# A pooling kernel whose engines are ordered by its own semaphores, with the framework's closing barriers placed after the first loads

## The chip, the cores and the metric

The kernel runs on one core of one Trainium2 chip. The metric is the device time of one execution in microseconds (us), the median of several runs. Five engines take part in a program, each with a queue of instructions of its own: TensorE (PE), VectorE (DVE), ScalarE (ACT), GpSimd (POOL) and SyncE (SP). The core's 16 DMA engines move data between the chip's memory (HBM) and the on-chip memory with its 128 partitions. Engines wait for one another, and for transfers, only through semaphores.

## What is computed

The reference is an adaptive average pool in one dimension. The input is float32 of 32 x 256 x 4096, the output 32 x 256 x 256, and each output is the mean of 16 neighbouring inputs:

```python
for i in range(output_size):
    start = int(i * length / output_size)
    end = int((i + 1) * length / output_size)
    result[:, :, i] = np.mean(x[:, :, start:end], axis=-1)
```

So 134.22 MB are read, 8.39 MB are written, and there is little arithmetic on each number.

## The kernel before

Batch and channel together make 8192 rows. A tile has 128 partitions with 4 rows each, so there are 16 tiles; one is 128 x 16384 numbers, 64 KB per partition. The first 15 tiles are cut so that a partition owns 60 rows that follow one another in memory (`x_many`, `o_many`, lines 46 and 47); the last tile has 4 rows per partition (`x_last`, `o_last`, lines 48 and 49).

One loop (line 56) runs over the tiles. Line 64, on SP's queue, loads a tile into one of two buffers (`inpool`, `bufs=2`, line 51). Each tile has 1024 windows of 16 numbers per partition, and two engines share them. POOL (line 67) folds the second 512 windows: it adds the upper 8 numbers of each to the lower 8, in place. DVE sums the first 512 windows whole (line 72) and then the folded ones (line 75). ACT (line 78) multiplies the 1024 sums by 1/16, in place, in the result tile. The results of 15 tiles stay on the chip in `res_many` and go out in one store (line 66), which stands on SP's queue behind the last load; those of the last tile are in `res_last` and go out in three stores (line 84), of 112, 8 and 8 partitions.

No semaphore is written in the kernel. The framework puts them in from the tiles that each instruction reads and writes: POOL and DVE wait for a load, DVE's second sum for POOL's fold, ACT for DVE, load t+2 for DVE's sums of tile t, the stores for ACT. Every transfer is issued by SP, whose queue is followed in order, so that an instruction that waits holds up all behind it.

The framework also frames the program. Line 101 opens it with a barrier over the five engines. Line 115, where the tile context ends, closes it: SP waits for each DMA semaphore (four wait instructions and a drain), then all engines meet in a barrier (each drains, raises a semaphore at POOL, and waits for POOL's release), POOL clears the framework's semaphores, and all engines meet in a second barrier. The profile puts a "q" behind an engine's name where it speaks of the engine's sequencer: SPq L115 is SP's part in this.

Of the kernel before, what the change touches and what calls it, by code (L numbers as in the profile page):

```python
# [1 line left out]

# [4 lines left out]


@with_exitstack
def kernel(  # L10
    ctx: ExitStack,
    tc: tile.TileContext,
    x: bass.AP,
    output_size: int,
    out: bass.AP,
):

    nc = tc.nc
    F32 = mybir.dt.float32
    X = mybir.AxisListType.X

    batch, channels, length = x.shape
    ob, oc, olen = out.shape
    assert ob == batch and oc == channels and olen == output_size
    assert length % output_size == 0
    window = length // output_size  # L30
    hw = window // 2
    inv_w = 1.0 / float(window)

    P = nc.NUM_PARTITIONS
    R = 4
    rows = batch * channels
    assert rows % (P * R) == 0
    ntiles = rows // (P * R)
    many = (ntiles - 1) * R
    cells = R * output_size  # L40
    m = cells // 2
    cols = R * length

    xr = x.rearrange("b c l -> (b c) l")
    orow = out.rearrange("b c o -> (b c) o")
    x_many = xr[0 : P * many, :].rearrange("(p r) l -> p (r l)", p=P, r=many)
    o_many = orow[0 : P * many, :].rearrange("(p r) o -> p (r o)", p=P, r=many)
    x_last = xr[P * many :, :].rearrange("(p r) l -> p (r l)", p=P, r=R)
    o_last = orow[P * many :, :].rearrange("(p r) o -> p (r o)", p=P, r=R)

    inpool = ctx.enter_context(tc.tile_pool(name="inpool", bufs=2))
    respool = ctx.enter_context(tc.tile_pool(name="respool", bufs=1))
    res_many = respool.tile([P, (ntiles - 1) * cells], F32, name="res_many")
    res_last = respool.tile([P, cells], F32, name="res_last")

    for t in range(ntiles):
        last = t == ntiles - 1
        xin = inpool.tile([P, cells, window], F32, name="xin")
        if last:
            res, base, src = res_last, 0, x_last  # L60
        else:
            res, base = res_many, t * cells
            src = x_many[:, t * cols : (t + 1) * cols]
        nc.sync.dma_start(out=xin.rearrange("p o w -> p (o w)"), in_=src)  # L64
        if last:
            nc.sync.dma_start(out=o_many, in_=res_many[:, :])
        nc.gpsimd.tensor_add(  # L67
            out=xin[:, m:cells, 0:hw],
            in0=xin[:, m:cells, 0:hw],
            in1=xin[:, m:cells, hw:window],  # L70
        )
        nc.vector.reduce_sum(  # L72
            out=res[:, base : base + m], in_=xin[:, 0:m, :], axis=X
        )
        nc.vector.reduce_sum(  # L75
            out=res[:, base + m : base + cells], in_=xin[:, m:cells, 0:hw], axis=X
        )
        nc.scalar.mul(  # L78
            out=res[:, base : base + cells],
            in_=res[:, base : base + cells],  # L80
            mul=inv_w,
        )
    for lo, hi in ((0, 112), (112, 120), (120, 128)):
        nc.sync.dma_start(out=o_last[lo:hi, :], in_=res_last[lo:hi, :])


# [1 line left out]
_INS = ['x', 'output_size']  # L88
_OUTS = [((32, 256, 256), 'float32')]

_NUMBERS = {'output_size': 256}


# [26 lines left out]
```

## Time and profile before

| What | Value |
|---|---|
| Time, median of 3 runs | 335.1 us (335.01 to 335.28) |
| Span of the profiled execution, first to last instruction of the program | 333.2 us |
| What lies around that span (335.1 - 333.2) | 1.9 us |
| Instructions in the profile | 160 |
| DVE busy | 209.7 us (63%) |
| POOL busy | 139.7 us (42%) |
| ACT busy | 18.2 us (5%) |

The time of the profiled execution is not listed apart from its span; what lies around the span is therefore taken from the median. It is the runtime's own work before and after the program, and no view of the profile shows it.

Reading: shares of busy time are means over the whole span. The timeline gives starts and durations in us from the span's start. A row of digits cuts the span, or the window asked for, into 40 equal slices, and a digit is the busy share of a slice in tenths (9 is 90% or more); in a short window a DMA packet counts in the slice in which it starts. The view of waits says who waited for whom: total, number of times, longest.

### The profile page before, as it was taken

To read this page: it belongs to the slowest core of one execution; us is meant where nothing else is said; L and a number is where in the kernel's file an instruction comes from. 1 tells how busy PE (TensorE), PEld (TensorE's weight loads), DVE (VectorE), ACT (ScalarE), POOL (GpSimd) and SP (SyncE) were. 2 spreads that over 40 slices of the span, in tenths; PEclk is the share of its full clock that TensorE was granted. 3 is DMA by queue.
4 is the path that set the end of the run, shared out by engine and by line. 5 is a ranking of instruction groups with operands and counts; after the bars stand their busy time and mean duration, and the time that the engine had idled before them with its cause. 6 is when DMAs were issued, how large, how long until landed. Compare 5 with 4: busy or idle time off the path is not lost.

```text
span 333.2 us, 160 instructions
## 1 busy us (share of the span) xinstructions
DVE 209.7 (63%) x32; ACT 18.2 (5%) x17; POOL 139.7 (42%) x20
## 2 busy tenths in 40 slices
DVE  0029396693929569392956839295783929578491
ACT  1000101000010100001010000101010010101001
POOL 0027091642709064370906336090733609073460
DMA  9898989999898989999898989999898989999997
GB/s 378 378 504 378 496 386 464 417 393 488 378 504 378 504 378 488 393 409 472 378 504 378 504 378 480 401 409 472 378 504 378 504 378 480 401 401 480 399 435 299
DMA packets 2608, 142.61 MB, mean 428 GB/s; under 512 B 304, under 2 KB 304, under 8 KB 432
## 3 DMA queue, kind: packets, MB, share of 16 engines
q1 hardware_dynamic: 2608, 142.61, 99.1%
HBM read 134.22 MB, written 8.39 MB: 428 GB/s over the span
## 4 chain that ended last, share of the span: by engine, by line
DMA 66%; POOL 18%; DVE 11%; POOLq 3%; issue 0%; ACT 0%; SPq 0%
DMA xin<-in_x_dram 66%; POOL xin L67 18%; DVE res_many L75 9%; POOLq L115 3%; DVE res_last L75 1%; ACT res_last L78 0%; SPq L64 0%; POOLq L67 0%
## 5 line engine op out<-in xcount | busy, mean ns | idle before, releaser
L67 POOL TENSOR_TENSOR xin<-xin 128x4096 f32<-128x4096 f32 x16 | 139.5, 8718 | 181.9 <-DMA xin<-in_x_dram 181.9
L72 DVE TENSOR_REDUCE res_many<-xin 128x512 f32<-128x8192 f32 x15 | 130.3, 8686 | 107.8 <-DMA xin<-in_x_dram 107.8
L75 DVE TENSOR_REDUCE res_many<-xin 128x512 f32<-128x4096 f32 x15 | 66.3, 4420 | 2.5 <-POOL xin L67 2.3
L78 ACT ACTIVATE res_many<-res_many 128x1024 f32<-128x1024 f32 x15 | 15.8, 1056 | 290.1 <-DVE res_many L75 290.1
L72 DVE TENSOR_REDUCE res_last<-xin 128x512 f32<-128x8192 f32 x1 | 8.7, 8686 | 6.1 <-DMA xin<-in_x_dram 6.1
L75 DVE TENSOR_REDUCE res_last<-xin 128x512 f32<-128x4096 f32 x1 | 4.4, 4420 | 0.2 <-POOL xin L67 0.2
L78 ACT ACTIVATE res_last<-res_last 128x1024 f32<-128x1024 f32 x1 | 1.1, 1056 | 18.3 <-DVE res_last L75 18.3
L78 ACT ACT_TABLE_LOAD x1 | 1.3, 1283 | 0.7 <-PEq L101 0.7
L101 POOL MEMSET const-float32-0.0<- 128x1 f32 x1 | 0.1, 98 | 0.2 <-issue 0.2
L101 POOL MEMSET const-bfloat16-1.0<- 128x1 bf16 x1 | 0.1, 101 | 0.0
L101 POOL MEMSET const-uint8-127<- 128x1 uint8 x1 | 0.1, 101 | 0.0
L101 POOL MEMSET const-float32-1.0<- 128x1 f32 x1 | 0.1, 98 | 0.0
## 6 DMA issues: line engine op xcount, KB each, us to landing
out_dram<-res_many SPq DMA_DIRECT2D x1, 7680.0 KB, 23.0
out_dram<-res_last SPq DMA_DIRECT2D x1, 448.0 KB, 4.8
xin<-in_x_dram SPq DMA_DIRECT2D x16, 25.4
out_dram<-res_last SPq DMA_DIRECT2D x2, 32.0 KB
```

The lines of the kernel that those rows point to most:

```text
L67: nc.gpsimd.tensor_add(out=xin[:, m:cells, 0:hw], in0=xin[:, m:cells, 0:hw], in1=xin[:, m:cells, hw:window],)
L72: nc.vector.reduce_sum(out=res[:, base : base + m], in_=xin[:, 0:m, :], axis=X)
L75: nc.vector.reduce_sum(out=res[:, base + m : base + cells], in_=xin[:, m:cells, 0:hw], axis=X)
L78: nc.scalar.mul(out=res[:, base : base + cells], in_=res[:, base : base + cells], mul=inv_w,)
L101: nc = _bacc.Bacc("TRN2", target_bir_lowering=False, num_devices=1)
L115: with _tile.TileContext(nc) as tc:
```

## The change

The tile pools go. The two load buffers and one result tensor (of the same total size) are allocated directly, and the kernel declares six semaphores: `landed0`, `landed1` for the loads into the two buffers, `folded` for POOL, `summed` for DVE, `scaled` for ACT and `stored` for the stores. The first two loads are issued inside the framework's critical section; directly behind it the kernel closes the tile context itself (`tc.close()`, `tc.compile()`), so that the framework's end of program (two barriers with POOL's clearing between them) comes at this place. All that follows is ordered by the new semaphores. The last tile's results go out in one store of 128 partitions. At the end SP clears five semaphores, waits for both stores, and clears the sixth; no barrier follows.

```diff
-    inpool = ctx.enter_context(tc.tile_pool(name="inpool", bufs=2))
-    respool = ctx.enter_context(tc.tile_pool(name="respool", bufs=1))
-    res_many = respool.tile([P, (ntiles - 1) * cells], F32, name="res_many")
-    res_last = respool.tile([P, cells], F32, name="res_last")
+    nbuf = 2
+    xin = [
+        nc.alloc_sbuf_tensor(f"xin{i}", [P, cells, window], F32, align_bytes=256)
+        for i in range(nbuf)
+    ]
+    res = nc.alloc_sbuf_tensor("res", [P, ntiles * cells], F32, align_bytes=256)
...
+    def load(t):
+        src = x_last if t == ntiles - 1 else x_many[:, t * cols : (t + 1) * cols]
+        dst = xin[t % nbuf][:, :, :].rearrange("p o w -> p (o w)")
+        nc.sync.dma_start(out=dst, in_=src).then_inc(landed[t % nbuf], 16)
...
+    with tc.tile_critical():
+        for t in range(nbuf):
+            load(t)
+    tc.close()
+    tc.compile()
 
     for t in range(ntiles):
...
+        xt = xin[t % nbuf]
+        lo, mid, hi = t * cells, t * cells + m, (t + 1) * cells
+        here = 16 * (t // nbuf + 1)
+
+        nc.gpsimd.wait_ge(landed[t % nbuf], here)
         nc.gpsimd.tensor_add(
...
-        )
+        ).then_inc(folded, 1)
+
+        nc.vector.wait_ge(landed[t % nbuf], here)
+        nc.vector.reduce_sum(out=res[:, lo:mid], in_=xt[:, 0:m, :], axis=X)
+        nc.vector.wait_ge(folded, t + 1)
         nc.vector.reduce_sum(
...
+            out=res[:, mid:hi], in_=xt[:, m:cells, 0:hw], axis=X
+        ).then_inc(summed, 1)
+
+        nc.scalar.wait_ge(summed, t + 1)
         nc.scalar.mul(
...
-    for lo, hi in ((0, 112), (112, 120), (120, 128)):
-        nc.sync.dma_start(out=o_last[lo:hi, :], in_=res_last[lo:hi, :])
+            out=res[:, lo:hi], in_=res[:, lo:hi], mul=inv_w
+        ).then_inc(scaled, 1)
+
+        if t + nbuf < ntiles:
+            nc.sync.wait_ge(summed, t + 1)
+            load(t + nbuf)
+
+    done = (ntiles - 1) * cells
+    nc.sync.wait_ge(scaled, ntiles - 1)
+    nc.sync.dma_start(out=o_many, in_=res[:, 0:done]).then_inc(stored, 16)
+    nc.sync.wait_ge(scaled, ntiles)
+    nc.sync.dma_start(out=o_last, in_=res[:, done:]).then_inc(stored, 16)
+    for s in (*landed, folded, summed, scaled):
+        nc.sync.sem_clear(s)
+    nc.sync.wait_ge(stored, 32)
+    nc.sync.sem_clear(stored)
```

As built, SP's queue holds after the opening barrier: a no-op that raises a semaphore, a branch to the critical section that waits for it, the two loads, four small instructions that leave the critical section, the two closing barriers, the other 14 loads, the two stores, five clears, and the clear of `stored` with its wait. On POOL, DVE and ACT the two barriers stand ahead of the first wait for a load, and their queues end with the last tile's work. Waits that stood as instructions of their own (SP and POOL had one for most tiles) are part of the instruction that waits.

More of the change, by code (lines that the diff above doesn't have):

```diff
@@ L49 @@
     o_last = orow[P * many :, :].rearrange("(p r) o -> p (r o)", p=P, r=R)
-    inpool = ctx.enter_context(tc.tile_pool(name="inpool", bufs=2))
-    respool = ctx.enter_context(tc.tile_pool(name="respool", bufs=1))
-    res_many = respool.tile([P, (ntiles - 1) * cells], F32, name="res_many")
-    res_last = respool.tile([P, cells], F32, name="res_last")
-    for t in range(ntiles):
[L57 to L70, printed above, removed]
-        )
[L72 to L82, printed above, removed]
@@ L83 @@
-    for lo, hi in ((0, 112), (112, 120), (120, 128)):
-        nc.sync.dma_start(out=o_last[lo:hi, :], in_=res_last[lo:hi, :])
+    nbuf = 2
[4 more added lines that the diff above has]
+    res = nc.alloc_sbuf_tensor("res", [P, ntiles * cells], F32, align_bytes=256)
+    landed = [nc.alloc_semaphore(f"landed{i}") for i in range(nbuf)]
+    folded = nc.alloc_semaphore("folded")
+    summed = nc.alloc_semaphore("summed")
@@ new lines @@
+    scaled = nc.alloc_semaphore("scaled")
+    stored = nc.alloc_semaphore("stored")
+    def load(t):
[7 more added lines that the diff above has]
+    tc.compile()
+    for t in range(ntiles):
+        xt = xin[t % nbuf]
+        lo, mid, hi = t * cells, t * cells + m, (t + 1) * cells
+        here = 16 * (t // nbuf + 1)
+        nc.gpsimd.wait_ge(landed[t % nbuf], here)
+        nc.gpsimd.tensor_add(
+            out=xt[:, m:cells, 0:hw],
+            in0=xt[:, m:cells, 0:hw],
+            in1=xt[:, m:cells, hw:window],
+        ).then_inc(folded, 1)
+        nc.vector.wait_ge(landed[t % nbuf], here)
+        nc.vector.reduce_sum(out=res[:, lo:mid], in_=xt[:, 0:m, :], axis=X)
+        nc.vector.wait_ge(folded, t + 1)
+        nc.vector.reduce_sum(
+            out=res[:, mid:hi], in_=xt[:, m:cells, 0:hw], axis=X
+        ).then_inc(summed, 1)
+        nc.scalar.wait_ge(summed, t + 1)
+        nc.scalar.mul(
+            out=res[:, lo:hi], in_=res[:, lo:hi], mul=inv_w
[3 more added lines that the diff above has]
+            load(t + nbuf)
```

## The prediction

> **What bounds the kernel now.** First the page: its DMA rows, its chain, and the groups.
>
> ```profile
> DMA  9898989999898989999898989999898989999997
> q1 hardware_dynamic: 2608, 142.61, 99.1%
> DMA xin<-in_x_dram 66%; POOL xin L67 18%; DVE res_many L75 9%; POOLq L115 3%; DVE res_last L75 1%; ACT res_last L78 0%; SPq L64 0%; POOLq L67 0%
> L67 POOL TENSOR_TENSOR xin<-xin 128x4096 f32<-128x4096 f32 x16 | 139.5, 8718 | 181.9 <-DMA xin<-in_x_dram 181.9
> L72 DVE TENSOR_REDUCE res_many<-xin 128x512 f32<-128x8192 f32 x15 | 130.3, 8686 | 107.8 <-DMA xin<-in_x_dram 107.8
> L75 DVE TENSOR_REDUCE res_many<-xin 128x512 f32<-128x4096 f32 x15 | 66.3, 4420 | 2.5 <-POOL xin L67 2.3
> out_dram<-res_many SPq DMA_DIRECT2D x1, 7680.0 KB, 23.0
> out_dram<-res_last SPq DMA_DIRECT2D x1, 448.0 KB, 4.8
> ```
>
> The transfers fill 99.1% of the 16 DMA engines' span, and POOL and DVE idle for data. The chain names POOL and DVE for 27%, but that is how it is followed: a load waits for the sums of its buffer, while the other buffer's load keeps the engines full. The sums in stretches say it plainly (columns: stretch, its length, DVE, ACT, POOL, clock, DMA share, GB/s).
>
> ```profile
> 22.70:312.90 290.20, 196.59 (x30) 15.84 (x15) 130.76 (x15) 1.00 1.00 433
> 1.70:332.20 330.50, 209.69 (x32) 17.21 (x17) 139.48 (x16) 1.00 1.00 431
> 332.20:333.20 1.00, 0.00 (x0) 0.00 (x0) 0.00 (x0) 1.00 0.00 0
> ```
>
> Between the first and the last landing of a load the share is 1.00 at 433 GB/s: 15 loads of 8.39 MB in 290.2 us, 19.35 us each. A tile's work takes 8.72 + 4.42 = 13.1 us, so a load is issued some 6 us before the engines need it. From 1.7 to 332.2 there is no hole at all, and then comes 1 us with nothing. The change can move three things: when the first load starts, how long the last store takes, and the end without transfers.
>
> **The middle: 0.** Semaphores in place of the framework's give the same order: POOL and DVE after a load, load t+2 after DVE's sums, stores after ACT. Those 6 us hide any difference in a wait; if the cover were gone, a late load would cost its lateness each time. SP's queue is passed by the closing barriers alone, behind the first two loads. As built, each engine has them ahead of its first wait for data, so SP is their last arrival, at about 1.6 us (two issues of 0.4 from 0.74 on); what they cost is bounded by the whole closing at the end, 1 us, and the first landing comes at 22.7 us: 20 us of cover.
>
> **The start: +0.2 us.** SP leaves the opening barrier and issues at once:
>
> ```profile
> L101 SPq EVENT_SEMAPHORE  x1: 17/17/17, 0.7 to 0.7; - x1
> 0.67 0.07 issue
> 0.74 0.41 SPq L64
> 1.14 0.06 issue
> 1.20 40.83 DMA xin<-in_x_dram
> ```
>
> The change puts a no-op and a branch, which waits for that no-op's semaphore, ahead of the first load. Since the DMA engines have no hole, a late start moves everything. No row shows such a branch. From below: two instructions at the 0.07 us that separate the wait and the issue, 0.14. From above: SP's longest wait in a closing barrier, a round through five engines, 0.4 (the last row of the next fence). I take 0.2, nearer the lower end, because this semaphore goes from SP to SP and meets no other engine. By the Trainium skill ("Advanced Engine Details and Errata", Control Flow Timing) a compare-and-branch takes about 108 ns; with it the estimate would be 0.07 + 0.11 = 0.18. No row here shows it.
>
> **The last store: +0.1 us.** The end of the trace, in the timeline, SP's waits, and SP's closing rows:
>
> ```profile
> 312.96 8.69 DVE L72 TENSOR_REDUCE res_last<-xin 128x512 f32<-128x8192 f32 x1 [6.06 <-DMA xin<-in_x_dram]
> 321.82 4.42 DVE L75 TENSOR_REDUCE res_last<-xin 128x512 f32<-128x4096 f32 x1 [0.17 <-POOL xin L67]
> 326.27 1.06 ACT L78 ACTIVATE res_last<-res_last 128x1024 f32<-128x1024 f32 x1 [18.28 <-DVE res_last L75]
> 327.36 1.52 SPq L84 DMA_DIRECT2D out_dram<-res_last  x3
> L115 SPq EVENT_SEMAPHORE  x6: 17/28/3282, 328.9 to 333.1; - x6
> SPq L115 <- DMA out_dram<-res_last: 3.3, 1, 3.3
> SPq L115 <- PEq L115: 0.6, 2, 0.4
> ```
>
> The last results are issued at 327.36, but the large store fills the engines until about 330: its packets are 7680 / 128 = 60 KB and take 2.26 us at 433 / 16 = 27 GB/s. The DMA view from 327 to the end shows the rest (a slice is 0.155 us, a packet stands where it starts):
>
> ```profile
> DMA  0000999990000000000269999998420000000000
> DMA packets 192, 1.51 MB, mean 243 GB/s; under 512 B 48, under 2 KB 48, under 8 KB 176
> ```
>
> Its last 16 packets start at 327.6 to 328.4, so they end at 329.9 to 330.7; the small rows follow from 329.8 on, without a hole. So issuing one store in place of three gains nothing by itself: 1.52 us of issue lie under the large store, and so does the making of the rows' descriptors (the first load had it done 1.0 to 1.7 us after its issue, by the same view of the start: issue at 0.74, packets from 1.75 to 2.5).
>
> ```profile
> DMA  0000000000000099900900000000000000000099
> ```
>
> What matters is how the 128 rows of 4 KB lie on the engines. At 128 x 4 KB / 423 GB/s (its plateau) they take 1.24 us, 0.155 us for one of the 8 on each engine. The 48 smallest packets, which raise semaphores, are 16 of the large store and 16 + 8 + 8 of the three small ones, so I read the two 8-row stores as lying on eight engines each. Rule and row meet here: the Trainium skill ("DMA: Bandwidth & Descriptors", Why a DMA increments its semaphore by 16 and not by 1) says that a transfer of 8 rows runs on the lowest-numbered 8 engines. By that rule, which speaks against the merge, before had 9 rows on eight engines and 7 on the other eight, where all now have 8; the count of 48 agrees with it, and which eight no row shows. Either way the price is one row: the 112-row store lands at 327.36 + 4.8 = 332.16, SP's wait for all ends at 328.93 + 3.28 = 332.21. If the 112-row store's last engine has 7 rows, it now gets an eighth and ends at 332.16 + 0.155 = 332.31: 0.1 later. Were they spread evenly before, nothing would change, and the sum below would be 0.1 lower. Bounds -0.15 and +0.15; I take +0.1, the value which the two landings, 0.05 apart, make likeliest.
>
> **The end: -0.9 us within the span, -0.2 after it.** Behind the landing at 332.21 come three more wait instructions, three drains, two barriers and POOL's clear, to 333.2: 0.99 us.
>
> ```profile
> L115 SPq DRAIN  x3: 7/7/7, 332.5 to 332.8; - x3
> L115 POOLq EVENT_SEMAPHORE_RANGE_CLEAR  x1: 95/95/95, 332.8 to 332.8; - x1
> ```
>
> All of it leaves the end. In its place stands one clear that carries the wait: 0.1 us by POOL's clear (SP's is not shown; between an SP instruction's 0.02 and 0.2). The other five clears stand behind the stores' issue, under some 4 us of flight; without that cover they would cost 5 x 0.1. That gives -0.89, bounds -0.97 and -0.79.
>
> Behind the span lies 335.1 - 333.2 = 1.9 us of the runtime's closing and launch. Before, all five engines come to it within 0.1 us of one another; now four of them have been there for over 5 us and only SP is late. If they meet once more there, part of the meeting is done beforehand. The nearest row is the meeting in the closing: two waits of SP for the others, 0.6 together, 0.4 the longer and so 0.2 the shorter. Bounds 0 and -0.4; I take -0.2, the middle. The Trainium skill ("Runtime: NRT & Kernel Launch", The launch sequence) has such a barrier pass through the engines in eight hops of 44 ns; four hops done beforehand would be an estimate of -0.18. No view shows it.
>
> **The sum.** +0.2 + 0.1 - 0.9 - 0.2 = -0.8. The page gives only the span (333.2) of the profiled execution; with the 1.9 around it, it is the median, 335.1. So 335.1 - 0.8 = **334.3 us**: the span falls to about 332.6. Lowest: +0.14 - 0.15 - 0.97 - 0.4 = -1.4, 333.7; highest: +0.4 + 0.15 - 0.79 = -0.24, 334.9.
>
> **The rivals.**
>
> *Given back at the start* (12%). The end saves its lower bound, 0.8, entering the critical section costs SP a full round, 0.4, the rows cost 0.15, and nothing is saved behind the span: 335.1 + 0.4 + 0.15 - 0.8 = 334.85. For it: no row prices that branch. Against it: SP alone takes part.
>
> *The branch stalls SP* (8%, and this one ends slower). If the jump makes SP's queue be read anew from memory, the first load waits for a read. Price: from an issue to the first packet 1.0 us, plus a landing; the shortest issue to landing in the page is 4.8, of which 2.6 are waiting behind the large store, so 1.0 to 2.2 us. In place of the 0.2 this gives 335.1 to 336.3; it decides above 1.7 us, where 335.8 is passed. I put it at 336.0. Against it: SP's queue is about 40 instructions long as built, and the branch goes to the instruction that stands next in it. The Trainium skill ("Runtime: NRT & Kernel Launch", Instruction fetch mechanics) says that a taken branch stalls if its target isn't in the window already fetched; no run here shows one.
>
> *The whole store is late* (4%). One store's descriptors need longer than three smaller ones' did, and the rows find the engines free before them. Cover is 329.8 - 327.36 - 1.7 = 0.8 us; past it each us counts in full. At 0.5 us past: 334.8.
>
> *The barriers stay in the way* (near 0): they would if they stood ahead of the loads, and the built order has them behind.
>
> **How the numbers follow.** The forecast has 76%. A measurement of this kernel can tell about 0.2%, 0.67 us, from no change; 334.43 is the border, close by. If the meeting behind the span gives nothing, the sum stands at -0.6 and is not told apart, but it would take the start above its value too to go far past that; of the 76 I give 68 to the faster side and 8 to the same. The first and third rival lie within 0.2%, the branch beyond: faster 0.68, same 0.24, slower 0.08. The range, 333.7 to 334.9, is that of the bounds and leaves out about 1 in 7.
>
> **What would show it.** Right: the first load issued near 0.9 us; the stretch from the first packet to the last still at a DMA share of 1.00 and some 19.35 us a load; 32 small packets at the end; SP's wait for the stores ending near 332.5, and the span 0.1 us behind it, near 332.6; the closing barriers before 5 us; the time falling by more than the span. Wrong: an issue above 1.2 us (the branch), a hole between the large store's packets and the rows (the late store), a hole between two loads (the middle), or a time that falls by less than the span.

## The result, and the profile after

| | Median | Lowest to highest | Span of the profiled execution |
|---|---|---|---|
| before | 335.14 us | 335.01 to 335.28 | 333.2 us |
| after | 333.64 us | 333.59 to 333.72 | 332.4 us |

The ratio is 0.9957, with a 95% interval of 0.9943 to 0.9971: 1.5 us faster. The forecast was 334.3 with a range of 333.7 to 334.9, so the direction came true and the time fell just below the range. The profiled execution after took 333.72 us, 1.3 us more than its span. The 1.9 that were reckoned before set a median against the span of another execution; in the 29 executions of the kernel before that were measured beside the first experiments, each with its own span to 0.1 us, the difference is 1.79 in the mean, and in the four executions after it is 1.30.

The middle first: two stretches as long as those of before, set 0.1 and 0.2 us later, from the sums in stretches of the kernel after (stretch, length, DVE, ACT, POOL, clock, DMA share, GB/s).

```profile
22.80:313.00 290.20, 196.58 (x30) 15.84 (x15) 130.80 (x15) 1.00 1.00 433
1.90:332.40 330.50, 209.69 (x32) 18.18 (x17) 139.52 (x16) 1.00 1.00 431
```

Share and rate are those of before, to the digit: 330.5 us of transfers without a hole, only 0.2 us later. All that the change moved lies ahead of them and behind them.

The start, in the chain of waits (start, duration, what) and in SP's rows:

```profile
0.67 0.05 issue
0.73 0.06 issue
0.79 0.03 SPq L71
0.82 0.12 issue
0.94 0.38 SPq L63
```
```profile
L71 SPq EVENT_SEMAPHORE  x2: 17/17/17, 2.3 to 2.7; - x2
L71 SPq COMPARE_BRANCH  x1: 33/33/33, 0.8 to 0.8; - x1
L71 POOLq EVENT_SEMAPHORE_RANGE_CLEAR  x1: 49/49/49, 2.4 to 2.4; - x1
```

The first load is issued at 0.94 instead of 0.74. The branch itself takes 0.03 us; with the no-op ahead of it and the 0.12 behind it, until the next instruction starts, entering the critical section costs 0.2. The Trainium skill ("Advanced Engine Details and Errata", Control Flow Timing) gives about 108 ns for a compare-and-branch; from its start to the load's it is 0.15 here. Both closing barriers are over at 2.7 us, 20 us ahead of the first landing.

The end, in the timeline, SP's waits, and SP's last two lines:

```profile
326.29 1.06 ACT L93 ACTIVATE res<-res 128x1024 f32<-128x1024 f32 x1 [18.61 <-DVE res L88]
327.38 0.34 SPq L105 DMA_DIRECT2D out_dram<-res  x1
```
```profile
SPq L109 <- DMA out_dram<-res: 4.4, 1, 4.4
SPq L71 <- PEq L71: 0.5, 2, 0.3
```
```profile
L107 SPq EVENT_SEMAPHORE_RANGE_CLEAR  x5: 25/30/39, 327.8 to 328.0; - x5
```
```profile
L109 SPq EVENT_SEMAPHORE_RANGE_CLEAR  x1: 25/25/25, 332.4 to 332.4; - x1
```

The five clears are done at 328.0, under the stores' flight. SP waits for the stores until 332.39, clears once, in 0.03 us, and the span ends at 332.42. Before, its wait ended at 332.21 and the span at 333.2. So within the span the landing is 0.18 us later and the rest 0.96 shorter: 0.8 less. The other part of the gain shows in no line of the program: it lies behind the span. Time minus span puts it at 0.5 us (1.79 and 1.30); the medians, less these 0.8, leave 0.7.

### The profile page after: what moved, and what is told of

It is laid out like the page before. It is cut to its first block, busy times and chain, and to the rows that moved or that the text cites. A ratio compares the mean times of both kernels' runs of the same rounds, so it can differ in the third digit from the quotient of the medians.

```text
span 332.4 us, 137 instructions
## 1 busy us (share of the span) xinstructions
DVE 209.7 (63%) x32; ACT 18.2 (5%) x17; POOL 139.7 (42%) x20
## 4 chain that ended last, share of the span: by engine, by line
DMA 66%; POOL 21%; DVE 11%; issue 0%; ACT 0%; SPq 0%
DMA xin<-in_x_dram 66%; POOL xin L79 21%; DVE res L88 11%; ACT res L93 0%; SPq L63 0%; SPq L71 0%; SPq L67 0%
## 5 line engine op out<-in xcount | busy, mean ns | idle before, releaser
L86 DVE TENSOR_REDUCE res<-xin 128x512 f32<-128x8192 f32 x16 | 139.0, 8686 | 114.8 <-DMA xin<-in_x_dram 114.8
L88 DVE TENSOR_REDUCE res<-xin 128x512 f32<-128x4096 f32 x16 | 70.7, 4420 | 1.8
L93 ACT ACTIVATE res<-res 128x1024 f32<-128x1024 f32 x16 | 16.9, 1056 | 306.4 <-DVE res L88 306.4
```

The lines of the kernel that those rows point to most:

```text
L86: nc.vector.reduce_sum(out=res[:, lo:mid], in_=xt[:, 0:m, :], axis=X)
L88: nc.vector.reduce_sum(out=res[:, mid:hi], in_=xt[:, m:cells, 0:hw], axis=X).then_inc(summed, 1)
L93: nc.scalar.mul(out=res[:, lo:hi], in_=res[:, lo:hi], mul=inv_w).then_inc(scaled, 1)
```

## Experiments

The theory of **arrival**: behind the program the runtime makes the five engines meet once more; each needs some time from its last instruction to that meeting, the engines differ in it, and the change gains there because four of them have long come. The rival, **weight**: what lies behind the span follows what the program leaves to close (barriers, semaphores, instructions), not when the engines come.

**All four engines held.** The changed kernel, with this at its end:

```diff
+    left = nc.alloc_semaphore("left")
+    nc.tensor.wait_ge(stored, 32)
+    nc.tensor.sem_inc(left, 1)
...
+    nc.sync.wait_ge(left, 4)
+    nc.sync.sem_clear(left)
     nc.sync.wait_ge(stored, 32)
     nc.sync.sem_clear(stored)
```

> The changed kernel (333.64 us, span 332.4), with PE, ACT, POOL and DVE held at the end of their queues until both stores have landed; each then raises one semaphore, for which SP waits before its last clears. Theory 'arrival': what lies behind the span is a meeting of the engines that the runtime adds, and each engine needs some time from its last instruction to it; the change gained behind the span because four engines had long come. Then time minus span goes from 1.3 us back to 1.7 to 1.9, the span grows by 0.1 to 0.2, and the time is 334.2 to 334.4. Rival 'weight': what lies behind the span follows what the program has to close (barriers, semaphores, instructions), not when the engines come. Then time minus span stays at 1.3 and only the span's growth is seen: 333.75 to 333.85.

Measured: 334.33 us, ratio to before 0.9979 (0.997 to 0.9988). The profiled execution took 334.07 with a span of 332.4: 1.7 around it. **POOL alone** held, and **PE alone** held, with the same lines for one engine:

> As the run with all four engines held, but POOL alone is held until both stores have landed. Theory 'arrival', with POOL as the slowest on its way to the meeting: nearly the whole loss of the run with four, 334.1 to 334.3, time minus span 1.7 to 1.9. Theory 'arrival' with all engines equally fast: SP comes last anyhow, and the time is 333.75 to 333.85. Rival 'weight': 333.75 too, with time minus span at 1.3.

> As the run with all four engines held, but PE alone is held until both stores have landed. Theory 'arrival' with POOL as the slow one: PE costs less than POOL, 333.8 to 334.0, time minus span 1.3 to 1.6. Rival 'weight': 333.75, the same as with POOL.

Measured: 334.46 with POOL (ratio 0.9981, 0.9972 to 0.999), 334.16 with PE (0.9976, 0.9965 to 0.9986). The page's first line and the held instruction's row (when its wait ended), first with POOL, then with PE:

```profile
span 332.6 us, 139 instructions
L110 POOLq EVENT_SEMAPHORE  x1: 17/17/17, 332.4 to 332.4; - x1
```
```profile
span 332.6 us, 139 instructions
L110 PEldq EVENT_SEMAPHORE  x1: 51/51/51, 332.4 to 332.4; - x1
```

Two programs with equally many instructions, equal spans, and one engine released at the same moment: the profiled executions took 334.33 and 334.16. With the spans to the hundredth (332.58 and 332.62), that is 1.75 around the span with POOL and 1.54 with PE, against 1.30 with neither. The means over all executions of each kernel say the same: 1.77 with POOL (11 executions), 1.54 with PE (7), 1.71 with all four (11), 1.30 with none (4). Weight would make POOL and PE equal, so it falls. The medians with POOL and with PE came out 0.16 above the top of what was expected. Part of that is the span, which grew more than expected (332.6 to 332.7 in the median with engines held, 332.35 after). The order is the expected one: POOL alone costs what four cost, 334.46 beside 334.33, and PE less.

The trace also holds the updates of the semaphores. Number 2, which no instruction of the kernels uses, is raised nine times as the engines come to the end of their work, and nine times again at the very end. The first five updates of the first nine, the end of SP's last instruction, and the last update of all, in us from the span's start:

```
             1st     2nd     3rd     4th     5th     SP's end   last of all
before     333.43  333.47  333.67  333.72  333.74     333.15      335.10
after        3.02  327.46  327.50  327.55  332.54     332.42      333.85
all held   332.51  332.55  332.77  332.81  332.84     332.36      334.20
POOL held    3.02  327.51  333.03  333.07  333.09     332.58      334.46
PE held    332.78  332.81  332.85  332.89  332.92     332.62      334.28
```

The engines pass this semaphore on in a fixed order. With PE held, the first update is late, and all after it; with POOL held, the third: so PE is first and POOL third, and SP, whose end the fifth follows in the kernel after, is the fifth. From the end of an engine's last instruction to its update PE takes 0.28 us (it ends at 332.50 where it is held), POOL 0.57 (332.46 where it is held), SP 0.12. From the fifth update to the last of all it is 1.31 us in the kernel after and 1.36 to 1.37 in the other four. So the time behind the program is settled by when the fifth update comes: 0.59 us after SP's end before, 0.12 after the change, which is 0.47 less. Before, POOL decides it: POOL ends at 333.11 and its update comes 0.56 later, at 333.67, when PE's has long come (333.43), and the fourth and fifth follow within 0.07.

From the end of the span, which before is PE's end, 0.05 us behind SP's, to the last update of all it is 1.90 us before and 1.43 after: these 0.47 us are the gain behind the span. (The last update stands 0.12 to 0.13 us behind the time of the same execution wherever both are on record.) The Trainium skill ("Runtime: NRT & Kernel Launch", The launch sequence) describes such a barrier, with 44 ns for a hop; the hops between engines that have already come, 0.02 to 0.05 us here, agree roughly. Each engine's way to the meeting, 0.12 to 0.57, is larger than a hop.

**The closing ahead of the first loads.** What does the place of the barriers bring?

```diff
-    with tc.tile_critical():
-        for t in range(nbuf):
-            load(t)
     tc.close()
     tc.compile()
+    for t in range(nbuf):
+        load(t)
```

> The changed kernel with the tile context closed before the first two loads instead of behind them, and without the critical section: the no-op and the branch go, and the closing barriers stand ahead of the first load. If the barriers cost at the start what SP's own rows behind the loads in the changed kernel show (about 0.95 us from its first drain to the last release): first load issued at about 1.6 us instead of 0.94, time 334.3. Rival: without the loads' issue ahead of them the two rounds are short, 0.4 us in all, and the no-op and the branch (0.2) are saved: 333.85.

```profile
L68 SPq DRAIN  x3: 7/7/7, 0.7 to 1.1; - x3
L68 SPq EVENT_SEMAPHORE  x2: 17/17/17, 1.0 to 1.3; - x2
```
```profile
1.39 0.86 SPq L63 DMA_DIRECT2D xin<-in_x_dram  x2
```

Measured: 334.16 us (ratio 0.9977, 0.9968 to 0.9985). The first load is issued at 1.39, 0.44 later than after the change, and the time is 0.5 longer: a late start is paid in full. It lies between the two expectations, since the barriers cost 0.65 us from the opening barrier to the issue, not 0.95. (The profiled execution of this kernel took 335.32, 1.2 above the median; only its start is read here.) Against before (335.05 in these runs) it is still 0.9 faster, with a first load issued 0.65 later: so having the barriers away from the end is worth some 1.5 us, and putting them behind the loads spares 0.44 of the 0.65 that they would cost at the start.

**Three last stores in the changed kernel**, and **one last store in the kernel before**:

```diff
-    nc.sync.dma_start(out=o_last, in_=res[:, done:]).then_inc(stored, 16)
+    for a, b in ((0, 112), (112, 120), (120, 128)):
+        nc.sync.dma_start(out=o_last[a:b, :], in_=res[a:b, done:]).then_inc(stored, 16)
...
-    nc.sync.wait_ge(stored, 32)
+    nc.sync.wait_ge(stored, 64)
```

> The changed kernel with the last tile's results again in three stores of 112, 8 and 8 partitions; the rest as changed (SP waits for all four stores). The prediction's step (the merged store lands 0.1 us later, since an engine that had 7 rows now has 8) gives 333.54. Rival: the engine that comes last is another one in each case, and the merge costs nothing: 333.64. With 32 small packets more or fewer nothing else differs.

> The kernel before with one last store of 128 partitions instead of three; nothing else of the change. The prediction's step gives 335.24 (0.1 us later). Rival, no cost of the merge: 335.14, or 0.1 to 0.15 less, since two issues of SP and two waits for landings leave the closing.

Measured: 333.61 with three stores (ratio to before 0.9959, 0.9947 to 0.9972; with one store it was 0.9957), and 334.95 for the kernel before with one store, where its own runs on that chip had 335.05 (ratio 0.9999, 0.999 to 1.0008). The intervals reach some 0.3 to 0.5 us to either side, so the times can neither show a price of 0.1 us nor rule it out. The packets of the two kinds, as the DMA view of the last 5.5 us shows them, first the kernel after, then with three stores:

```profile
DMA packets 176, 1.51 MB, mean 274 GB/s; under 512 B 32, under 2 KB 32, under 8 KB 160
```
```profile
DMA packets 192, 1.51 MB, mean 274 GB/s; under 512 B 48, under 2 KB 48, under 8 KB 176
```

The counts are as forecast, 32 and 48 small packets. The traces also hold the start and duration of every packet, and these part what the times can't. From the end of the large store's last packet to the start of the last small one, then to the last update of a store's semaphore, in us:

```
                         to the last    to the last
                         small packet   update        together
before, three stores        1.09          0.51          1.60
before, one store           1.24          0.46          1.70
changed, three stores       1.09          0.46          1.55
changed, one store          1.24          0.35          1.59
```

The eighth row is there: 0.155 us more until the last small packet, in both kernels. But the update follows that packet sooner with one store, most of all in the changed kernel. Together the merge costs 0.10 us in the kernel before and 0.04 in the changed one, and from before to after nothing. These are single executions (0.35 recurs in the kernels with held engines and with the clears moved), and why the update comes sooner was not tried. In the kernel before the time hides the 0.10, since SP has one wait left behind the last landing instead of three: from the last update to the end of the span it is 1.01 us with three stores and 0.87 with one.

**The clears behind the wait.**

```diff
-    for s in (*landed, folded, summed, scaled):
-        nc.sync.sem_clear(s)
     nc.sync.wait_ge(stored, 32)
-    nc.sync.sem_clear(stored)
+    for s in (*landed, folded, summed, scaled, stored):
+        nc.sync.sem_clear(s)
```

> The changed kernel with the five clears moved behind SP's wait for the stores. In the changed kernel they stand 0.06 us apart under the stores' flight. If the end of SP's queue sets the end of all: span and time 0.3 us longer, 333.95. Rival: SP's end is hidden behind the runtime's own closing, and the time stays at 333.64 while the span grows by 0.3.

```profile
L108 SPq EVENT_SEMAPHORE_RANGE_CLEAR  x6: 25/28/34, 332.4 to 332.7; - x6
```

Measured: 334.02 us, 0.4 longer, with a span 0.3 longer and 1.3 around it in the profiled execution (333.99). SP's end sets the end of all: five instructions of 0.03 us behind the last wait, 0.06 apart, cost 0.3 to 0.4. So the order of the waits and clears at the end is worth more than the no-op and the branch at the start cost (0.2).

**A first load in parts**, meant to start the last DMA engine sooner and so to beat both kernels:

```diff
+        if t == 0:
+            nc.sync.dma_start(out=dst[0:16], in_=src[0:16]).then_inc(landed[0], 16)
+            nc.sync.dma_start(out=dst[16:P], in_=src[16:P]).then_inc(landed[0], 16)
+            return
...
-        here = 16 * (t // nbuf + 1)
+        here = 16 * (t // nbuf + 1 + (t % nbuf == 0))
```

> The changed kernel with its first load in two: 16 partitions, then 112. The DMA engines have no hole from the first packet to the last, but in the changed kernel's records their first packets start over a stretch of some 0.6 us. Theory: that spread comes from making 8 descriptors for each engine in turn; with one for each engine the last engine starts 0.3 to 0.5 us sooner, the second part's descriptors come under the first packets of 3 us, and the time falls to 333.2 to 333.4. Rival: the spread has nothing to do with the number of rows, or the engines share a limit so that the sum of bytes alone counts: 333.64. A third way: the 112 rows come late and leave a hole: slower.

Measured: 354.43 us, ratio 1.0577 (1.0563 to 1.0592), 19 us slower than before, in a way that none of the three expected: the transfers themselves are slow. From the sums in stretches, first the kernel after while its first load is under way, then with the split load:

```profile
5.00:22.00 17.00, 0.00 (x0) 0.00 (x0) 0.00 (x0) 1.00 1.02 443
```
```profile
5.00:40.00 35.00, 0.00 (x0) 0.00 (x0) 0.00 (x0) 1.00 0.88 210
```

By the traces' packets, the first 16 of 64 KB took 8.5 us each and the 112 behind them 4.6 in the median; in the kernel after the first 16 took 3.1 and those behind them 2.4.

Four more kernels cut the first load in eight transfers of 16 partitions, and part the chip's side from the input's:

```diff
+        if t == 0:
+            for k in range(8):
+                nc.sync.dma_start(
+                    out=dst[k:P:8], in_=src[k:P:8]
+                ).then_inc(landed[0], 16)
+            return
...
-        here = 16 * (t // nbuf + 1)
+        here = 16 * (t // nbuf + 1 + 7 * (t % nbuf == 0))
```

In place of `k:P:8` stands `16 * k : 16 * k + 16` on both sides, on the chip's side, or on the input's.

> The changed kernel with its first load in eight transfers of 16 partitions, each taking every eighth partition (k, k + 8, ...), so that the 16 rows of a transfer are spread over the whole chip memory and the whole input. In the run with the first load split in 16 and 112 partitions, the packets of 64 KB of the 16 neighbouring partitions took 8.5 us where 3.0 are usual. Theory 'neighbours': rows that lie side by side, in the input or on the chip, share something, and 16 engines at once on 16 neighbours go at a third of the pace; then this split goes at the usual pace, the first landing comes near 22.8 us, and the time is 333.4 to 333.8. Rival 'short transfers': a transfer with one row for each engine is slow wherever its rows lie; then the first landing comes at some 70 us and the time is near 380.

> As the run with every eighth partition, but each of the eight transfers takes 16 neighbouring partitions (0 to 15, 16 to 31, ...), which are neighbouring rows of the input too (0.98 MB apart). Theory 'neighbours': 8.5 us for each transfer, first landing near 70 us, time near 380. If only the very first transfer of a program is slow, the first landing comes near 29 us and the time is about 340.

> As the run with 16 neighbouring partitions, but each group of 16 is filled with every eighth row of the input, so the rows are neighbours on the chip only. The first tile's rows come in another order than in the reference; the work is the same. If the neighbours matter on the chip: slow as with neighbouring partitions, near 380. If they matter in the input: the usual pace, 333.4 to 333.8.

> The other half: each transfer fills every eighth partition with 16 neighbouring rows of the input, so the rows are neighbours in the input only. The first tile's rows come in another order than in the reference; the work is the same. If the neighbours matter on the chip: the usual pace, 333.4 to 333.8. If they matter in the input: near 380.

Measured: 354.54 us with every eighth partition on both sides, 387.06 with neighbours on both, 387.31 with neighbours on the chip alone, 354.80 with neighbours in the input alone; the last three are a single execution each. The stretch from 5 to 40 us, in this order:

```profile
5.00:40.00 35.00, 0.00 (x0) 1.28 (x1) 0.00 (x0) 1.00 1.02 210
```
```profile
5.00:40.00 35.00, 0.00 (x0) 1.28 (x1) 0.00 (x0) 1.00 1.06 120
```
```profile
5.00:40.00 35.00, 0.00 (x0) 1.28 (x1) 0.00 (x0) 1.00 1.05 120
```
```profile
5.00:40.00 35.00, 0.00 (x0) 1.28 (x1) 0.00 (x0) 1.00 1.02 210
```

The last column decides. Neighbouring partitions on the chip make it 120 GB/s, whatever the rows of the input; every eighth partition makes it 210, again whatever the input. By the traces a packet of 64 KB takes 9.2 us with neighbours and 5.1 with every eighth partition. So the neighbours matter on the chip only. But 210 is still half of what the whole load of 128 partitions reaches (433), so neither theory alone is right. That having one row for each engine makes a transfer slow is not shown either: the 112 rows of the first split are seven for each of 16 engines, and their packets took 4.6 us. Whether it is the set of partitions that the engines fill at one moment was not parted from the size of the transfer, and the factor of two stays open.

## Why the prediction was right or wrong

**The middle (0)** was right: the stretch between the first and the last landing is 290.2 us in both (DVE starts on them at 22.73 and 312.96 before, at 22.82 and 313.05 after), and the closing barriers are over at 2.7 us.

**The start (+0.2)** was right: 0.94 against 0.74. That such a delay is paid in full was shown by the closing ahead of the loads, 0.44 later and 0.5 longer. The rival in which the branch stalls SP fell: 0.03 us for the branch and 0.12 behind it.

**The last store (+0.1)** came out at nothing: SP's wait ended 0.18 later, which the start explains alone. The row was read rightly. From the end of the large store's last packet to the last small packet it is 1.09 us with three stores and 1.24 with one, that is seven and eight times 0.155, so the engine that comes last had seven rows and now has eight. What failed is the rest of the step, that the landing follows the rows at the same distance: it came 0.51 us behind the last small packet before and 0.35 after, and that gives the row back. It is not so in every kernel, as the table above shows. The third rival, a late store, did not come about: the first rows start at 330.27, when the first of the large store's last packets ends. (Its cover, 329.8 - 327.36 - 1.7, is 0.74 us rather than 0.8.)

**The end within the span (-0.9)** was right: 0.99 us became 0.03, that is -0.96. SP's clear took 0.03, where POOL's 0.1 had been put down.

**Behind the span (-0.2, bounds 0 and -0.4)** is the step that failed, in size and not in mechanism. The meeting is there and part of it is now done beforehand, but it was priced by SP's waits in the program's own closing barriers, 0.2 and 0.4, and these do not show an engine's way out of the program. On the way to the runtime's meeting POOL needs 0.57 us and PE 0.28, against SP's 0.12, and before the change POOL's way stood at the end. By the updates the gain is 0.47, and by time minus span 0.49: beyond the bound of 0.4.

Summed again with the measured terms: +0.2 + 0.0 - 0.96 - 0.47 = -1.2. The profiled executions agree: the last updates are 335.10 and 333.85, 1.25 apart. From 335.1 that gives 333.9, inside the range, so the mis-sized term alone doesn't account for the whole miss. The medians are 1.5 apart in the first comparison and 1.4 with the medians of before in the later ones (335.05), and with the 0.2 to 0.3 left over the time fell 0.06 us below the range. They lie within the spans: the spans of the 29 executions before average 333.29 and those of the four after 332.35, which is 0.94 apart, where the two profiled ones are 0.78 apart. Executions of one kernel differ by about as much, and no run assigns this rest to a step.

## What to carry to other kernels

When one resource is busy from its first use to its last, the time of a kernel is that stretch plus what stands ahead of it and behind it, and there every sequencer instruction counts in full: 0.06 us each here. Put synchronisation that must happen once where the resource is already busy, and let the end hang on one engine, one wait, one instruction. Choose that engine by how fast it gets out of the program: here SP (0.12 us) rather than PE (0.28) or POOL (0.57).

## What the runs showed of the hardware that was not expected

A DMA share of 1.00 says that the engines have packets, not how fast they move bytes: in the first loads cut in eight the share was 1.02 to 1.06 at 120 or 210 GB/s, against 1.00 at 433 for transfers of 128 partitions. With a load of 128 rows of 64 KB cut into transfers of 16 partitions, the kernel took 53 us longer with neighbouring partitions (387 against 333.6 us) and 21 us longer with every eighth. Why the same 128 rows in one transfer show neither loss is open.
